# A decoder trunk on one core: softmax rows transposed without scaling, their inverse sums brought through memory into the output gates

## The chip, the cores and the metric

The kernel runs on one core of one Trainium2 chip. The metric is the device time of one execution in microseconds (us). The engines are TensorE (PE: matrix products and transposes), VectorE (DVE), ScalarE (ACT), GpSimd (POOL) and SyncE (SP), whose queue issues nearly all DMA transfers. Each engine works off its own instructions in order and waits for others through semaphores.

## The reference, cut to what matters

The network has two layers on a sequence of 512 tokens with 1024 channels, in float32. Layer 0 mixes tokens with a gated MLP, layer 1 with "forgetting attention"; behind each stands an MLP with squared ReLU. The change is in layer 1's attention:

```python
p = h @ w_in                       # q | k | v | gate | forget logits
q, k = rms_norm(q, q_g), rms_norm(k, k_g)        # per head, 16 heads of 64
c = cumsum(log_sigmoid(f_logit + b_f))           # per head, over tokens
logits = q @ k.T * 64**-0.5 + c[t] - c[s]        # masked to s <= t
probs = softmax(logits)
o = (probs @ v) * sigmoid(gate)
x = x + o @ w_out
```

A softmax row is exp(logit - max) divided by the sum of the row. The division can be made on the row itself, or later on the row's sum of values, since it is one number for each token and head.

## The kernel before, in words

**Products.** Each float32 factor is split into a high part (rounded to the matrix format, by ACT) and a low part (the rest, by DVE or POOL), and a product is three matmuls: high x high, high x low, low x high. Weights come from memory in chunks of up to 512 KB: a raw buffer (three of them), then the split into `wh` (L85, ACT) and `wl` (L86, in the attention stage on POOL). The class `Stream` loads chunks ahead of their use through SP's queue (L80).

**Stages.** The gated MLP layer, its MLP, the attention, the second MLP. The attention runs from about 630 to 922 us of the profile and works on pairs of heads, p = 0 to 7, with head 2p + e and e = 0, 1.

**One pair** is the generator `attend` (L758). The projections `project` (L691) have made q, k and v for all tokens; `attend` turns q and k (L765), scales and splits them (L771 to L775, the low parts on DVE), and then for each of the two heads:

- loads the head's cumulated forget values from memory into all partitions, `cb` (L785, 256 KB, a tag with two buffers), and adds them to the token's own value on POOL: the tiles `bias` (L792, and the causal mask L794), one for each block i of 128 query tokens;
- for i = 0 to 3 makes the negated logits of (i + 1) * 128 keys in PSUM (`lg`), adds the bias and takes the row's minimum on DVE (L803), and takes the exponential with the row's sum `sm` on ACT (L804);
- takes the reciprocal `rc` of the four sums (L806) and scales the four blocks `ee` with it (L808), on DVE.

When both heads are there, and the pair's gates too (`gates[p]`, 128 x 512: the channels of both heads by tokens, from `gate_act`, L729), the blocks are transposed on PE by L840 into PSUM (`tp`), and split into `pth` (ACT, L842) and `ptl` (DVE, L843). `values` (L817) multiplies them with v (PSUM tile `ot`), adds the two halves into `z` (L826 on ACT, L827 on DVE), and multiplies with the gates (L828). The result is split once more (L859, L860) for the output projection.

**What sets the order.** PE's order in the attention stage is written out. The projections of later pairs, the gates and the output products are the main line (`FOX_ORDER`, L35); after each small step of it, `advance` (L866) lets one running `attend` make its next step if its due time has come. A due time is PE time as the program adds it up (`order["us"]`, L239) plus a lag given by the generator at each `yield`: `LAG_SOFT` between the last logits and the first transpose, `LAG_PT` after each set of transposes, and so on. PE's instructions are kept in this order. The instructions of DVE, ACT, POOL and SP are put in order by a scheduler that simulates the whole program; each engine then holds to it. PSUM tiles tagged B (three buffers) serve `lg`, `tp` and the turned q and k alike.

Of the kernel before, what the change touches and what calls it, by code (L numbers as in the profile page):

```python
# [8 lines left out]
F32 = mybir.dt.float32  # L9
F32R = mybir.dt.float32r  # L10
AF = mybir.ActivationFunctionType
ALU = mybir.AluOpType
# [4 lines left out]
P = 128  # L17
D = 1024
S = 512
KB = D // P  # L20
NT = S // P
E = 2 * D
FF = 4 * D
H = 16
DH = 64
# [113 lines left out]
def trunk(ctx: ExitStack, tc: tile.TileContext, A, out, stages=4):  # L139
    nc = tc.nc  # L140
    pe, dve, act, pool = nc.tensor, nc.vector, nc.scalar, nc.gpsimd
# [6 lines left out]
    dram = ctx.enter_context(tc.tile_pool(name="dram", bufs=1, space=DRAM))  # L148
# [4 lines left out]
    def psB(name):  # L153
        return ps.tile([P, S], F32, tag="B", name=name, bufs=3)

    def psD(name):
        return ps.tile([P, S], F32, tag="D", name=name, bufs=1)
# [83 lines left out]
    def mm(dst, a, b, start, stop, more=False):  # L241

        ins = pe.matmul(dst, a, b, start=start, stop=stop, skip_group_check=more)  # L243
        placed(ins, dst.shape[-1])
        return ins

    def turn(dst, src):
        placed(pe.transpose(dst, src, ident[: src.shape[0], : src.shape[0]]), 256)  # L248
# [357 lines left out]
    with ExitStack() as st:  # L606
        fs = st.enter_context(tc.tile_pool(name="fs", bufs=2))
        fp = st.enter_context(tc.tile_pool(name="fp", bufs=2))
# [12 lines left out]
            dve.memset(kl[e][(1 - e) * DH : (2 - e) * DH].bitcast(F32), 0.0)  # L621
        ct = fp.tile([P, NT, H], F32, tag="ct", name="ct", bufs=1)
        cd = dram.tile([H, S], F32, tag="cd", name="cd")

        def forget(pq):

# [30 lines left out]
        gates, vals, o = {}, {}, {}  # L657
# [33 lines left out]
        def project(p, values=True):  # L691
# [33 lines left out]
            pool.tensor_tensor(sf, sf, mhalf, op=ALU.pow)  # L725
            dve.tensor_tensor(yh, yh, sf.unsqueeze(2).to_broadcast([P, NT * 4, DH]), op=ALU.mult)  # L726
            running.append([order["us"] + LAG_NORM, attend(p, y), None])

        def gate_act(p, pg):  # L729
# [28 lines left out]
        def attend(p, y):  # L758

            if p:  # L760
                yield 0.0, ("L", p - 1, 1)
            tq, tk = (psB(f"t{w}{p}") for w in "qk")
            for c, t in enumerate((tq, tk)):
                for i in range(NT):
                    turn(t[:, i * P : (i + 1) * P], y[:, i, c * P : (c + 1) * P])  # L765

            qs, ks = ([fp.tile([P, S], F32R, tag=f"{w}s{e}", name=f"{w}s{p}_{e}") for e in range(2)] for w in "qk")
            own = [slice(0, DH), slice(DH, P)]
            for e in range(2):
                a, b = own[e], own[1 - e]  # L770
                act.activation(qs[e][a], tq[a], AF.Copy, scale=qkn[a])  # L771
                act.activation(ks[e][a], tk[a], AF.Copy, scale=qkg[a, 1:2])
                act.activation(ks[e][b], tk[a], AF.Copy, scale=qkg[a, 1:2])
                dve.scalar_tensor_tensor(qs[e][b], tq[a], qkn[a], qs[e][a].bitcast(F32), op0=ALU.mult, op1=ALU.subtract)
                dve.scalar_tensor_tensor(kl[e][a], tk[a], qkg[a, 1:2], ks[e][a].bitcast(F32), op0=ALU.mult, op1=ALU.subtract)  # L775
            did.add(("Q", p))
            rush = LAST if p > 6 else 1.0
            lag = LAG_QK * rush
            soft = []
            for e in range(2):  # L780
                hd = 2 * p + e
                yield lag, ("T", p - 1, e) if p else "F"
                lag = 0.0
                cb = fp.tile([P, S], F32, tag="cb", name=f"cb{hd}")
                nc.sync.dma_start(cb, cd[hd].partition_broadcast(P))  # L785
                ees = []
                sm = fs.tile([P, NT], F32, tag="sm", name=f"sm{hd}")
                mn = fs.tile([P, NT], F32, tag="mn", name=f"mn{hd}")
                for i in range(NT):
                    n = (i + 1) * P  # L790
                    bi = fp.tile([P, n], F32, tag=f"bias{i}", name=f"bias{hd}_{i}", bufs=1)
                    pool.tensor_scalar(bi, cb[:, :n], 1.0, ct[:, i, hd : hd + 1], op0=ALU.mult, op1=ALU.add)  # L792
                    dg = bi[:, i * P :]
                    pool.affine_select(dg, dg, pattern=[[-1, P]], compare_op=ALU.is_ge, fill=BIG, base=0, channel_multiplier=1)  # L794
                    yield lag, None
                    lag = LAG_LOGIT * rush
                    ee = fp.tile([P, n], F32, tag=f"ee{i}", name=f"ee{hd}_{i}", bufs=2)
                    ees.append(ee)
                    lg = psB(f"lg{hd}_{i}")
                    ts_ = slice(i * P, (i + 1) * P)  # L800
                    mm(lg[:, :n], qs[e][:, ts_], ks[e][:, :n], True, False)
                    mm(lg[:, :n], qs[e][:, ts_], kl[e][:, :n], False, True)
                    dve.tensor_tensor_reduce(ee, lg[:, :n], bi, 1.0, 3.0e38, op0=ALU.add, op1=ALU.min, accum_out=mn[:, i : i + 1])  # L803
                    act.activation(ee, ee, AF.Exp, bias=mn[:, i : i + 1], scale=-1.0, accum_out=sm[:, i : i + 1])  # L804
                rc = fs.tile([P, NT], F32, tag="rc", name=f"rc{hd}")
                dve.reciprocal(rc, sm)  # L806
                for i in range(NT):
                    dve.tensor_scalar(ees[i], ees[i], rc[:, i : i + 1], None, op0=ALU.mult)  # L808
                soft.append(ees)
                did.add(("L", p, e))  # L810
            yield LAG_SOFT * rush, ("G", p)
            if p in (4, 5):
                yield 0.0, ("W", 0)
            weights = []
            z = fp.tile([P, S], F32, tag="oz", name=f"oz{p}")

            def values(e):  # L817

                ot = psD(f"ot{2 * p + e}")
                for j in range(NT):  # L820
                    both = vals[p][:, j, 2 * e : 2 * e + 2].rearrange("p w d -> p (w d)")
                    for w in range(2):
                        mm(ot[:, j * P :], both, weights[e][j][w], j + w == 0, j + w == NT)
                    if j < NT - 1:
                        yield 0.0, None
                act.activation(z[own[e]], ot[own[1 - e]], AF.Copy)  # L826
                dve.tensor_tensor(z[own[e]], ot[own[e]], z[own[e]], op=ALU.add)  # L827
                dve.tensor_tensor(z[own[e]], z[own[e]], gates[p][own[e]], op=ALU.mult)  # L828

            for e in range(2):  # L830
                hd = 2 * p + e
                ph = fp.tile([P, TRI], F32R, tag="pth", name=f"pth{hd}", bufs=2)
                pl = fp.tile([P, TRI], F32R, tag="ptl", name=f"ptl{hd}", bufs=2)
                at = 0
                weights.append([])
                for j in range(NT):
                    n = (NT - j) * P
                    tp = psB(f"tp{hd}_{j}")
                    for i in range(j, NT):
                        turn(tp[:, (i - j) * P : (i - j + 1) * P], soft[e][i][:, j * P : (j + 1) * P])  # L840
                    sl = slice(at, at + n)
                    act.activation(ph[:, sl], tp[:, :n], AF.Copy)  # L842
                    dve.tensor_tensor(pl[:, sl], tp[:, :n], ph[:, sl].bitcast(F32), op=ALU.subtract)  # L843
                    weights[e].append((ph[:, sl], pl[:, sl]))
                    at += n
                    yield LAG_PT * rush, None
                did.add(("T", p, e))
                if e:
                    yield 0.0, ("V", p)
                    yield from values(0)  # L850
                    yield LAG_PV * rush, None
                    yield from values(1)
            if p < 6:
                h = fp.tile([P, S], F32R, tag="oh", name=f"oh{p}", bufs=4)
                l = fp.tile([P, S], F32R, tag="ol", name=f"ol{p}", bufs=4)
            else:
                h = xp.tile([P, S], F32R, tag=f"xh{p}", name=f"oh{p}")
                l = xp.tile([P, S], F32R, tag=f"xl{p}", name=f"ol{p}")
            act.activation(h, z, AF.Copy)  # L859
            dve.tensor_tensor(l, z, h.bitcast(F32), op=ALU.subtract)  # L860
            o[p] = (h, l)
            did.add(("O", p, 1))
# [113 lines left out]
```

## Time and profile before

| | us |
|---|---|
| median of 3 runs | 1277.02 (1276.41 to 1278.97) |
| the profiled execution | 1277.01 |
| its span in the trace | 1275.3 |
| PE busy | 1262.1 (99%) |
| DVE busy | 877.2 (69%) |
| ACT busy | 624.9 (49%) |
| POOL busy | 484.7 (38%) |
| DMA, mean | 97 GB/s |

The span is what the trace covers; the rest of the profiled execution's time lies around it. Busy times are sums over the whole span and hide the stages. A row of a group gives the line, the engine, the operation, the tiles (written <- read), and its times; "idle before" is the time for which the engine stood before the instruction, with what ended it. The granted clock of TensorE was full throughout.

### The profile page before, as it was taken

How to read it: one execution, taken by the hardware profiler on the slowest of the kernel's cores; microseconds unless marked ns; L12 is line 12 of the kernel's file. 1: busy time of each engine (PE TensorE's matmuls, PEld its weight loads, DVE VectorE, ACT ScalarE, POOL GpSimd, SP SyncE). 2: the span in 40 equal slices, each digit the busy share in tenths (PEclk: the TensorE clock that was granted, in tenths of full speed). 3: DMA queues.
4: the chain of work that ended last, by engine and by line, in shares of the span. 5: the costliest groups of instructions: out<-in, count | busy, mean ns of one | idle time of the engine just before them, and what ended most of it. 6: DMA issues, size and time to landing. Idle time of an engine off the chain costs nothing.

```text
span 1275.3 us, 18354 instructions
## 1 busy us (share of the span) xinstructions
PE 1262.1 (99%) x7108; PEld 1114.0 (87%) x7108; DVE 877.2 (69%) x1206; ACT 624.9 (49%) x981; POOL 484.7 (38%) x415
## 2 busy tenths in 40 slices
PE   9999999999999999999999999999999999999998
PEld 7888888888999999998899899898888999999987
DVE  7347767677867676765537777777887767676763
ACT  7334423246534344443467687678465444444430
POOL 4108433025423232310657667667173322323200
PEclk9999999999999999999999999999999999999999
DMA  7333233233233332323223222223223323232321
GB/s 250 97 107 92 83 91 91 84 98 93 90 116 100 100 102 97 111 89 96 80 81 103 84 82 76 84 77 106 83 67 116 116 84 116 84 116 83 118 81 66
DMA packets 39607, 124.01 MB, mean 97 GB/s; under 512 B 4816, under 2 KB 5840, under 8 KB 39520
## 3 DMA queue, kind: packets, MB, share of 16 engines
q1 hardware_dynamic: 39232, 122.82, 30.4%
q8 instruction: 56, 0.92, 0.3%
q14 instruction: 31, 0.25, 0.1%
q10 hardware_dynamic: 288, 0.02, 0.0%
HBM read 120.69 MB, written 2.13 MB: 96 GB/s over the span
## 4 chain that ended last, share of the span: by engine, by line
PE 89%; DVE 6%; ACT 2%; issue 1%; POOL 1%; DMA 1%; DVEq 0%; ACTq 0%; POOLq 0%
PE po L243 36%; PE da L243 11%; PE bc L243 9%; PE pq L243 8%; PE pv L243 8%; PE pu L243 7%; PE ph L243 3%; PE pg L243 2%; PE ot L243 2%; DVE xl L271 1%; PE lg L243 1%; PE tp L248 1%; PE sp L426 1%; DVE ee L808 1%; DVE y L726 1%
## 5 line engine op out<-in xcount | busy, mean ns | idle before, releaser
L85 ACT ACTIVATE wh<-raw 128x1024 fp32r<-128x1024 f32 (+3 forms) x230 | 219.7, 957 | 270.9 <-PE po L243 83.5
L86 DVE TENSOR_TENSOR wl<-raw,wh 128x1024 fp32r<-128x1024 f32 (+1 forms) x178 | 252.5, 1432 | 46.2 <-ACT wh L85 45.4
L243 PE MATMUL po<-zl,wh 128*128 128x512 f32 x512 | 200.6, 392 | 1.3 <-DVE zl L500 1.3
L243 PE MATMUL po<-zh,wh 128*128 128x512 f32 x512 | 199.9, 391 | 0.0
L243 PE MATMUL po<-zh,wl 128*128 128x512 f32 x512 | 199.5, 390 | 0.0
L556 DVE TENSOR_TENSOR x<-x,po 128x512 f32<-128x512 f32 x128 | 87.2, 683 | 106.1 <-PE po L243 106.1
L86 POOL TENSOR_TENSOR wl<-raw,wh 128x768 fp32r<-128x768 f32 (+3 forms) x52 | 102.4, 1969 | 125.7 <-ACT wh L85 123.2
L110 POOL TENSOR_TENSOR ssum<-raw 128x512 f32<-128x512 f32 x26 | 35.5, 1364 | 268.6 <-DMA raw<-in_m_dram 256.8
L85 ACT ACTIVATE sh<-ssum 128x1024 fp32r<-128x1024 f32 x52 | 55.2, 1061 | 164.5 <-POOL ssum L111 95.8
L243 PEld LDWEIGHTS po<-zh,wl 128*128 128x128 f32 x512 | 96.2, 188 | 19.5
L243 PEld LDWEIGHTS po<-zh,wh 128*128 128x128 f32 x512 | 96.5, 188 | 17.9
L243 PEld LDWEIGHTS po<-zl,wh 128*128 128x128 f32 x512 | 96.6, 189 | 17.8 <-DVE zl L500 1.6
L243 PE MATMUL pq<-wh,xh 128*128 128x384 f32 (+2 forms) x256 | 88.4, 345 | 0.0
L410 POOL TENSOR_SCALAR vn<-v,mv,lnr 128x128 f32<-128x128 f32 x64 | 63.1, 999 | 59.5 <-DVE vl L414 59.4
L243 PE MATMUL pq<-wh,xl 128*128 128x384 f32 (+2 forms) x256 | 83.1, 325 | 0.0
L243 PE MATMUL pq<-wl,xh 128*128 128x384 f32 (+2 forms) x256 | 82.7, 323 | 0.0
L86 DVE TENSOR_TENSOR sl<-ssum,sh 128x1024 fp32r<-128x1024 f32 x52 | 65.9, 1268 | 18.2 <-ACT sh L85 18.1
L112 POOL TENSOR_TENSOR ssum<-raw,ssum 128x512 f32<-128x512 f32 x26 | 37.1, 1428 | 69.1 <-DVE sl L86 68.8
L243 PE MATMUL da<-th,sl 128*128 128x256 f32 x208 | 58.9, 283 | 0.0
L243 PE MATMUL da<-tl,sh 128*128 128x256 f32 x208 | 58.8, 283 | 0.0
L243 PE MATMUL pv<-wh,xh 128*128 128x512 f32 (+1 forms) x160 | 58.0, 372 | 0.7 <-ACT wh L85 0.7
L243 PE MATMUL pv<-wl,xh 128*128 128x512 f32 (+1 forms) x160 | 58.7, 368 | 0.0
(212 smaller groups left out, 3489.9 us busy)
## 6 DMA issues: line engine op xcount, KB each, us to landing
raw<-in_m_dram SPq DMA_DIRECT2D x128, 512.0 KB, 3.6
raw<-in_gw_u_dram SPq DMA_DIRECT2D x16, 512.0 KB, 3.5
raw<-in_gw_o_dram SPq DMA_DIRECT2D x16, 512.0 KB, 3.5
raw<-in_fw_qkv_dram SPq DMA_DIRECT2D x20, 384.0 KB, 3.0
raw<-in_gw_v_dram SPq DMA_DIRECT2D x14, 512.0 KB, 3.9
raw<-in_fw_g_dram SPq DMA_DIRECT2D x8, 512.0 KB, 3.4
cb<-cd SPq DMA_DIRECT2D x16, 256.0 KB, 3.3
raw<-in_fw_o_dram SPq DMA_DIRECT2D x8, 512.0 KB, 3.5
```

The source lines that it names most:

```text
L85: self.nc.scalar.activation(hi, t, AF.Copy)
L86: eng.tensor_tensor(lo, t, hi.bitcast(F32), op=ALU.subtract)
L110: tt(s12[:, 0], a21, a22, op=ALU.add)
L112: tt(s43[:, 0], a12, s12[:, 1], op=ALU.subtract)
L243: ins = pe.matmul(dst, a, b, start=start, stop=stop, skip_group_check=more)
L248: placed(pe.transpose(dst, src, ident[: src.shape[0], : src.shape[0]]), 256)
L271: dve.scalar_tensor_tensor(l, x[b], gcol, h.bitcast(F32), op0=ALU.mult, op1=ALU.subtract)
L410: pool.tensor_scalar(vn[:, i], v[i][:, cb * P : (cb + 1) * P], mv[:, i, 0:1], lnr[:, i : i + 1], op0=ALU.subtract, op1=ALU.mult)
L426: pe.matmul(dst, vh[:, 2 * c + i], wide, start=True, stop=False)
L556: dve.tensor_tensor(x[b], x[b], pt, op=ALU.add)
L726: dve.tensor_tensor(yh, yh, sf.unsqueeze(2).to_broadcast([P, NT * 4, DH]), op=ALU.mult)
L808: dve.tensor_scalar(ees[i], ees[i], rc[:, i : i + 1], None, op0=ALU.mult)
```

## The change

The four scalings of a head (L808) go. The blocks are transposed and split as the exponential left them, and the values are summed with these weights. The reciprocals of both heads of a pair are put in one tile `rc` (128 tokens x 2 heads x 4 blocks), and one DMA on SP's queue writes them to memory (`rd`, 16 heads x 512 tokens) so that a head's 512 values lie in a row: 1024 single values of four bytes. After the wait for the pair's gates, two DMAs on SP's queue read the two rows back, each into the 64 partitions of its head: the tile `rb` (128 x 512), which takes its buffers from the tag `cb`. After the transposes of the second head, DVE multiplies the pair's gates with `rb`, and `values` uses these gates as before. No lag is changed.

```diff
+        rd = dram.tile([H, S], F32, tag="rd", name="rd")
...
             soft = []
+            rc = fs.tile([P, 2, NT], F32, tag="rc", name=f"rc{p}")
             for e in range(2):
...
-                rc = fs.tile([P, NT], F32, tag="rc", name=f"rc{hd}")
-                dve.reciprocal(rc, sm)
-                for i in range(NT):
-                    dve.tensor_scalar(ees[i], ees[i], rc[:, i : i + 1], None, op0=ALU.mult)
+                dve.reciprocal(rc[:, e], sm)
                 soft.append(ees)
                 did.add(("L", p, e))
+
+            with nc.allow_non_contiguous_dma(reason="1024 values"):
+                nc.sync.dma_start(rd[2 * p : 2 * p + 2].rearrange("e (i t) -> t e i", t=P), rc)
             yield LAG_SOFT * rush, ("G", p)
+            rb = fp.tile([P, S], F32, tag="cb", name=f"rb{p}")
+            for e in range(2):
+                nc.sync.dma_start(rb[own[e]], rd[2 * p + e].partition_broadcast(DH))
             if p in (4, 5):
                 yield 0.0, ("W", 0)
...
                 did.add(("T", p, e))
                 if e:
+                    dve.tensor_tensor(gates[p], gates[p], rb, op=ALU.mult)
                     yield 0.0, ("V", p)
                     yield from values(0)
```

## The prediction

> **What bounds the kernel now.** The page first: which engine is busy, and what the chain that ended last consists of.
>
> ```profile
> span 1275.3 us, 18354 instructions
> PE 1262.1 (99%) x7108; PEld 1114.0 (87%) x7108; DVE 877.2 (69%) x1206; ACT 624.9 (49%) x981; POOL 484.7 (38%) x415
> ...
> PE 89%; DVE 6%; ACT 2%; issue 1%; POOL 1%; DMA 1%; DVEq 0%; ACTq 0%; POOLq 0%
> ```
>
> TensorE is the bound: 1262.1 of 1275.3 us, and 89% of the chain. Work on DVE counts only where it holds PE up, and DVE is on the chain for 6%. So I looked at the stretch that the change touches, one window for each pair of heads, and at PE's idle time in it: the stretch's length less PE's busy time. (Columns: the window and its length; busy time of PE, weight loads, DVE, ACT and POOL with their instructions; granted clock, share of the DMA engines, GB/s. Eight windows; the four left out are the quiet ones.)
>
> ```profile
> 668.00:698.00 30.00, 29.58 (x182) 28.45 (x182) 21.83 (x49) 21.92 (x49) 22.95 (x28) 1.00 0.35 110
> 698.00:730.00 32.00, 29.42 (x174) 27.18 (x173) 23.57 (x53) 22.64 (x51) 19.95 (x22) 1.00 0.24 71
> ...
> 851.00:878.00 27.00, 26.18 (x191) 24.11 (x189) 21.02 (x47) 21.45 (x46) 18.59 (x23) 1.00 0.29 89
> 878.00:922.00 44.00, 43.37 (x236) 36.41 (x235) 35.41 (x77) 25.34 (x52) 17.50 (x14) 1.00 0.28 91
> sum 254.00, PE 249.27 PEld 226.75 DVE 191.46 ACT 183.07 POOL 159.00; mean PE 31.16 PEld 28.34 DVE 23.93 ACT 22.88 POOL 19.88
> ```
>
> PE idles 254.00 - 249.27 = 4.73 us in the whole stretch, at a granted clock of 1.00. 2.58 of it lie in the second window, 0.82 in the seventh, 0.63 in the last and 0.42 in the first; the other four have 0.3 together. This is the largest part of the argument: however much DVE is relieved, about 4.7 us (0.37%) can come back. PE's ends are modelled, so a little more may hide in "busy"; I allow 1 us.
>
> Then who made PE wait. First PE's waits over the whole trace, next PE's own timeline, then the chain of waits around the same place and one piece of it later on (columns: start, length, what).
>
> ```profile
> PE tp L248 <- DVE ptl L843: 3.6, 4, 1.9
> ```
>
> ```profile
> 714.78 0.30 PE L248 MATMUL tp<-ident,ee 128*128 128x128 f32 x1 [1.87 <-DVE ptl L843]
> ...
> 718.13 0.44 PE L248 MATMUL tp<-ident,ee 128*128 128x128 f32 x2 [0.71 <-DVE ptl L843]
> ```
>
> ```profile
> 681.61 1.08 DVE ee L808 x3
> ...
> 708.18 1.69 DVE ee L808 x3
> ...
> 712.16 1.27 DVE ee L808 x4
> ...
> 715.43 2.44 DVE y L726
> ...
> 864.09 2.42 DVE ee L808 x4
> ```
>
> The transposes' PSUM buffers (three) come free when DVE has made the low part `ptl`, and DVE is late with it since the scalings of L808 stand ahead of it: 1.08 us on the chain in the first window, 1.69 + 1.27 in the second, 2.42 in the seventh. These scalings are what the change removes. Ahead of the second wait (0.71) stands a product of the projections, `y` L726, which stays.
>
> **The change part by part.**
>
> *Removed:* 64 scalings, 8 in each pair. Their busy time over the same eight windows, their durations (least/median/most), and those of the product nearest to what is added:
>
> ```profile
> sum 254.00, DVE 28.64; mean DVE 3.58
> L808 DVE TENSOR_SCALAR ee<-ee,rc x64: 272/470/1510, 674.7 to 895.1; 128x128 f32<-128x128 f32 x16, 128x256 f32<-128x256 f32 x16, 128x384 f32<-128x384 f32 x16, 128x512 f32<-128x512 f32 x16
> L860 DVE TENSOR_TENSOR ol<-oz,oh x8: 683/731/1719, 700.9 to 917.4; 128x512 fp32r<-128x512 f32 x8
> ```
>
> So 28.64 us leave DVE, 3.58 per pair. The 16 reciprocals stay.
>
> *Added on DVE:* 8 products of 128x512 (gates times `rb`). The nearest row is L860, two SBUF inputs of the same shape: 683 ns at least, 731 at the median, 1719 at most. I take 0.73: 5.8 us, bounds 5.5 and 13.8. DVE's net relief is 22.8 us (14.8 to 23.1).
>
> The spread of L808 (272 to 1510 ns) and L860 (683 to 1719) shows DVE instructions being held up now and then. The Trainium skill, page "SBUF — State Buffer", section "Who interferes with whom", has a rule for it: VectorE and GpSimd share one pair of ports, an exclusive lock. By it a product with two SBUF inputs is exposed to POOL's work, so 1.72 rather than 0.73 would be the price: the relief 14.8 and not 22.8 us.
>
> *Moved:* the transposes no longer wait for reciprocal and scaling but for the exponential alone. Their place in PE's order doesn't change: it is written out by the lags, and those are untouched. So a transpose can't start earlier than its turn; only the waits found above can shrink.
>
> *What of the 4.73 us goes.* First window 0.42: 1.08 of scaling is on its chain; gone. Second: the 1.87 goes whole (2.96 us of scaling precede it on DVE), the 0.71 behind `y` L726 by half: 2.2. Seventh: 2.42 us of scaling precede, then other DVE work; half: 0.4. Last: 0.6. Sum 3.6 us. What is late next there is `y` L726 and ACT, which makes the high part.
>
> *Added on the queues:* for each pair one write of 1024 single values (4 KB) to memory and two broadcasts back, 64 partitions of 2 KB each (128 KB). No row shows a write of single values; the nearest DMA rows (KB each, median us from issue to landing):
>
> ```profile
> DMA packets 39607, 124.01 MB, mean 97 GB/s; under 512 B 4816, under 2 KB 5840, under 8 KB 39520
> ...
> cb<-cd SPq DMA_DIRECT2D x16, 256.0 KB, 3.3
> ...
> wsT<-in_w_sT_dram SPq DMA_DIRECT2D x1, 512.0 KB, 3.9
> cd<-cs SPq DMA_DIRECT2D x1, 32.0 KB, 2.0
> ```
>
> `cd<-cs` writes 16 rows in 2.0 us, the lower bound. `wsT` moves 128 x 8 rows of 512 B (the 5840 - 4816 = 1024 packets between the two sizes) in 3.9: as many packets as the new write has, only far fuller; the upper bound. I take 3.0. The two broadcasts together move what one `cb<-cd` moves in 3.3, and the second issue adds an estimated 0.4; below, the 2.0 of the small write, and 0.4. I take 3.0. From the last reciprocal of a pair, R, the sums are back at R + 6.0 us (4.4 to 7.6, the sums of the bounds).
>
> *Who waits for them.* The product waits on DVE, in order; behind it stand the `ptl` of the transposes and the next pair's work, and PE waits for these. The pair at 742 us on DVE:
>
> ```profile
> 743.40 0.18 DVE L806 RECIPROCAL rc<-sm 128x4 f32<-128x4 f32 x1 [0.64 <-ACT ee L804]
> ...
> 749.03 1.72 DVE L843 TENSOR_TENSOR ptl<-tp,pth 128x512 fp32r<-128x512 f32 x4 [0.42 <-ACT pth L842]
> 754.64 0.68 DVE L827 TENSOR_TENSOR oz<-ot,oz 64x512 f32<-64x512 f32 x1 [3.89 <-ACT oz L826]
> 755.36 0.68 DVE L828 TENSOR_TENSOR oz<-oz,gt 64x512 f32<-64x512 f32 x1
> ```
>
> R is 743.6. The gates are needed at 755.4, R + 11.8, and DVE idles from 750.7 to 754.6, R + 7.2 to R + 11.1. In program order the product comes right behind that last `ptl`: the sums (R + 6.0) are there, and the product lies in the hole and costs nothing. If DVE's order has it earlier, where the scheduler thought the sums were back, DVE stands for a microsecond or two with `ptl` behind it. PE's idle time per DVE time has been 4.73 / 28.64 = 0.17; 8 pairs x 0.5 us x 0.17 = 0.7 us lost. I take 0.5.
>
> The Trainium skill, page "DMA: Bandwidth & Descriptors", section "Specifications", speaks against this write: below 512 B a transfer does read-modify-write. If that doubles what `wsT` takes above the 2.0 us of the small write, the new one takes 5.8 us, 2.8 more than I took, and if all of it were DVE standing, the sum would be 8 x 2.8 x 0.17 = 3.8 us higher, 1277.7 us: the gain gone. No row of before shows such a write, and the hole of 3.9 us covers the 2.8; 0.04 of the chance of "nothing to be measured" (below) is for it.
>
> *SP.* Its queue stands waiting most of the time, each load for a buffer:
>
> ```profile
> SPq L80 <- POOL wl L86: 188.7, 39, 7.1
> ```
>
> A write put behind such a load comes later, by 188.7 / 39 = 4.8 us on average; a load put behind the write or the broadcasts comes later by the 3.0 us for which the broadcasts wait. The weights are three raw buffers ahead of their use, and PE's waits name no load; I cost it at nothing. Without that cover it is 3 us in a pair, 24 in all.
>
> **Sum.** The profiled execution took 1277.01 us (span 1275.3 and 1.7 around it), the median of the runs is 1277.02: the same. 1277.0 - 3.6 + 0.5 = 1273.9 us, -0.24%. About 0.2% (2.6 us) is what a measurement of this kernel can tell from no change, so the forecast is only just "faster".
>
> **The rivals.**
>
> *B, nothing to be measured.* PE's order is fixed and four of eight windows have no idle time to give. If ACT and `y` L726 are late anyway, only the 1.87 shrinks, by half, and the first 0.42 goes: 1277.0 - 1.4 = 1275.6. For it: the 0.71 stands behind `y`. Against it: 2.96 us of scaling stand ahead of a wait of 1.87.
>
> *C, slower: the sums come late, and DVE stands at the product.* In SP's order the write gets behind a load that waits 4.8 us; back at R + 10.8 while DVE came to it at R + 6. The rate: at 3.58 us of scaling per window, DVE's lateness cost PE 2.58 in the second window and 0.3 in each of the others. 4.8 us per pair then costs 0.4 to 3.5; in the middle 1.9, 8 pairs 15.5 us: 1277.0 - 3.6 + 15.5 = 1289 (1277 to 1301). With half the pairs hit, 1281. It decides from 3.58 - 0.73 = 2.9 us of standing per pair, where DVE loses what it gained. For it: SP's waits, and the unseen write of single values. Against: the hole of 3.89 us, and 4.4 to 7.6 against 11.8.
>
> *D, the forget rows come late.* `rb` shares the two buffers of `cb`, so the second head's `cb` of the next pair can load only once the product is done, 3.3 us before its first use. Tightest here (POOL, then DVE):
>
> ```profile
> 820.87 0.37 POOL L792 TENSOR_SCALAR bias<-cb,ct 128x128 f32<-128x128 f32 x1
> ```
>
> ```profile
> 827.63 0.28 DVE L803 CUSTOM_DVE_ANT_0 ee<-lg,bias 128x128 f32<-128x128 f32 x1
> ```
>
> That pair's last `ptl` ends near 822; product 822.7, `cb` landed 826.0, bias 0.7 later: 0.9 us before DVE wants it at 827.63. Each microsecond beyond that is PE's once three buffers of logits are full. With the sums 2 us late in all seven pairs that have a successor, about 1 us each: 1273.9 + 7 = 1281.
>
> **Chances.** The forecast 0.50 (its own range 1271.3, all 4.73 and 1 more gone, to 1275.5), B 0.27, C 0.16, D 0.07. Of the forecast 0.42 lie below 1274.5 and 0.08 above; B is "same", C and D "slower". So faster 0.42, same 0.35, slower 0.23. The range reaches below to 1270.5 and above to 1284, into C.
>
> **What would show it.** Right: PE's wait for `ptl` falls from 3.6 us to under 1, PE's idle time in the stretch to 1 to 2 us, DVE loses some 23 us, and no wait of DVE on a DMA `rb` over 1 us. The write lands in 2.0 to 3.9 us. Wrong: a row of DVE waiting for `rb` with several microseconds (C); POOL waiting for `cb` (D); DVE 23 us lighter with PE's idle time as before (B).

## The result and the profile after

The changed kernel takes 1360.97 us at the median of four executions (three of 1360.18 to 1361.32 and a disturbed one of 6354.67; without that one the median is 1360.62), the kernel before 1277.18 in the same job. The ratio, without the disturbed execution, is 1.0652, interval 1.0631 to 1.0673: 83.8 us slower by the medians, where 3.1 us faster was forecast. The profiled execution took 1360.18 us.

The page of the kernel after, the same lines as before:

```profile
span 1358.4 us, 18347 instructions
PE 1279.0 (94%) x7108; PEld 1129.7 (83%) x7108; DVE 854.7 (63%) x1150; ACT 624.6 (46%) x981; POOL 484.3 (36%) x415
...
PE 79%; DMA 7%; DVE 5%; issue 3%; ACT 2%; POOL 2%; SPq 0%; DVEq 0%; POOLq 0%; ACTq 0%
```

The span grew by 83.1 us. PE's idle time went from 1275.3 - 1262.1 = 13.2 to 1358.4 - 1279.0 = 79.4 us, 66.2 more; its busy time grew by 16.9 for the same 7108 matmuls. 66.2 + 16.9 = 83.1: the whole loss, in two parts. DMA, 1% of the chain before, is now 7%. DVE is 22.5 us lighter (877.2 to 854.7), as meant.

The waits of the attention stage (who waited <- for whom: us in all, how often, longest), and the DMA issues of the tiles concerned (KB each, median us from issue to landing):

```profile
DVE gt L854 <- DMA rb<-rd: 76.0, 8, 10.7
POOL bias L794 <- DMA cb<-cd: 73.6, 8, 10.5
...
PE tp L248 <- DVE ptl L848: 62.5, 10, 9.6
...
PE pq L243 <- DVE x L325: 9.2, 1, 9.2
```

```profile
cb<-cd SPq DMA_DIRECT2D x16, 256.0 KB, 3.8
...
rb<-rd SPq DMA_DIRECT2D x16, 128.0 KB, 4.6
...
rd<-rc SPq DMA_DIRECT2D x8, 4.0 KB, 9.0
```

DVE stands at the new product in all eight pairs, 9.5 us on average, and PE stands behind it: 62.5 us for a `ptl`, where it was 3.6, and in the fifth pair 9.2 us for an `x` (L325), which DVE makes right behind the product there. The write of 4 KB takes 9.0 us to land at the median, longer than any other transfer here; the loads of 64 times its size take 3.8. The first pair on DVE, and then the chain of waits at the same place:

```profile
680.39 0.18 DVE L807 RECIPROCAL rc<-sm 128x4 f32<-128x4 f32 x1 [0.62 <-ACT ee L806]
...
683.50 0.88 DVE L848 TENSOR_TENSOR ptl<-tp,pth 128x384 fp32r<-128x384 f32 x2
694.30 0.69 DVE L854 TENSOR_TENSOR gt<-gt,rb 128x512 f32<-128x512 f32 x1 [9.92 <-DMA rb<-rd]
694.91 0.88 DVE L848 TENSOR_TENSOR ptl<-tp,pth 128x128 fp32r<-128x128 f32 x2
```

```profile
680.60 9.34 DMA rd<-rc
689.95 0.51 SPq L816
690.51 3.69 DMA rb<-rd
694.30 0.69 DVE gt L854
695.25 0.69 PE tp L248 x2
```

The last reciprocal ends at R = 680.57. The sums are back at 694.2, R + 13.6. DVE's order has the product after three of the eight `ptl`, at R + 3.8 (684.38), with five `ptl` of the same pair behind it. PE needs these to free its PSUM buffers, so it stands too. In the other pairs the product comes after none to four of the eight.

What PE does around that stall (columns as in the prediction; the granted clock comes after the engines):

```profile
684.40:694.30 9.90, 1.90 (x14) 1.54 (x12) 0.00 (x0) 2.01 (x3) 2.17 (x1) 0.73 0.23 54
689.10:699.10 10.00, 3.85 (x13) 3.75 (x14) 3.69 (x7) 0.66 (x2) 3.55 (x5) 0.50 0.43 118
699.30:726.00 26.70, 24.77 (x145) 22.82 (x144) 17.64 (x38) 20.01 (x45) 17.38 (x18) 1.00 0.23 65
```

While DVE stands (first row, DVE 0.00) PE finds 1.90 us of work. In the second row the granted clock is 0.50 for 10 us; PE starts again at 695.25 and does 3.85 us of matmuls in it at half speed, of which about half, 1.9, is lost. There is such a stretch of half clock in each of the eight pairs, and PE is busy for 36.6 us in all of them together; half of that, 18.3 us, is close to the 16.9 by which PE's busy time grew. From 699.3 the clock is 1.00 again. The Trainium skill, page "TensorE: Matmul & The Clock Gate", Part 1, says that the gate goes back to half speed after about 3.4 us of idling and opens after as long a busy time; the trace agrees roughly: the granted clock is half from 689.0, 2.7 us after PE's last matmul (it ends at 686.3), and full again from 699.2, 4.0 us after PE's restart. It is full throughout the attention of the kernel before, whose longest wait for a `ptl` was 1.9 us.

### The profile page after: what moved, and what is told of

Same layout as the page of the kernel before. It is cut to its first block, busy times and chain, and to the rows that moved or that the text cites. A ratio compares the mean times of both kernels' runs of the same rounds, so it can differ in the third digit from the quotient of the medians.

```text
span 1358.4 us, 18347 instructions
## 1 busy us (share of the span) xinstructions
PE 1279.0 (94%) x7108; PEld 1129.7 (83%) x7108; DVE 854.7 (63%) x1150; ACT 624.6 (46%) x981; POOL 484.3 (36%) x415
## 4 chain that ended last, share of the span: by engine, by line
PE 79%; DMA 7%; DVE 5%; issue 3%; ACT 2%; POOL 2%; SPq 0%; DVEq 0%; POOLq 0%; ACTq 0%
PE po L243 32%; PE da L243 11%; PE bc L243 8%; PE pv L243 7%; PE pu L243 6%; PE pq L243 6%; DMA rd<-rc 5%; PE ph L243 2%; DMA rb<-rd 2%; PE pg L243 2%; DVE xl L271 1%; PE ot L243 1%; POOL wl L86 1%; PE lg L243 1%; PE sp L426 1%
## 5 line engine op out<-in xcount | busy, mean ns | idle before, releaser
L243 PE MATMUL pq<-wh,xh 128*128 128x384 f32 (+2 forms) x256 | 92.2, 360 | 9.2 <-DVE x L325 9.2
L248 PE MATMUL tp<-ident,ee 128*128 128x128 f32 x160 | 32.2, 303 | 62.5 <-DVE ptl L848 62.5
L243 PE MATMUL pq<-wh,xl 128*128 128x384 f32 (+2 forms) x256 | 86.1, 336 | 0.0
L243 PE MATMUL pq<-wl,xh 128*128 128x384 f32 (+2 forms) x256 | 86.0, 336 | 0.0
L248 PEld LDWEIGHTS tp<-ident,ee 128*128 128x128 f32 x160 | 22.4, 154 | 70.2 <-DVE ptl L848 66.1
L794 POOL TENSOR_SCALAR bias<-cb,ct 128x128 f32<-128x128 f32 (+1 forms) x64 | 38.9, 618 | 83.5 <-DMA cb<-cd 73.6
L847 ACT ACTIVATE pth<-tp 128x512 fp32r<-128x512 f32 (+1 forms) x64 | 27.2, 433 | 87.9 <-PE tp L248 87.8
```

## The experiments

**Theory 1:** the scattered write is slow, DVE stands at the product for it, in order, ahead of the `ptl` that PE needs. **Theory 2:** the transfers hurt without the product: `rb` takes a buffer of `cb`, and the broadcasts stand in SP's queue waiting for the write, so the forget rows come late (73.6 us of POOL waiting for `cb`). The first three runs tell these apart.

### No inverse at all

```diff
-            with nc.allow_non_contiguous_dma(reason="1024 values"):
-                nc.sync.dma_start(rd[2 * p : 2 * p + 2].rearrange("e (i t) -> t e i", t=P), rc)
...
-            rb = fp.tile([P, S], F32, tag="cb", name=f"rb{p}")
-            for e in range(2):
-                nc.sync.dma_start(rb[own[e]], rd[2 * p + e].partition_broadcast(DH))
...
-                    dve.tensor_tensor(gates[p], gates[p], rb, op=ALU.mult)
```

> The changed kernel without the write of the inverse sums, their way back and the product with the gates: the division by the rows' sums is left out, so this is the ceiling of what the missing scalings can bring. By the forecast's term (3.6 us of PE's idle time come back, nothing added): 1273.4 us, PE's wait for ptl under 1 us. By rival B (ACT and the product y are late anyway): 1275.6 us. If the missing scalings themselves disturbed the order: above 1277.

Measured: 1275.01 us (1272.10 to 1276.53), ratio 0.9977 (0.9968 to 0.9986). Removing the scalings alone is worth 2.2 us; 3.6 was forecast. PE's waits for `ptl` are not shorter than the 3.6 us of before, and a long `y` product of the projections stands where the scalings were (waits, then DVE's timeline; the profiled execution took 1276.37 us):

```profile
PE tp L248 <- DVE ptl L841: 4.1, 3, 2.2
```

```profile
712.55 3.34 DVE L726 TENSOR_TENSOR y<-y,yss 128x1024 f32<-128x1024 f32 x1
```

So 27.6 us less work on DVE (877.2 to 849.6) buys 2.2; the 83.8 us come from what is added, not from what the transposes now carry.

### The transfers without the product

```diff
-                    dve.tensor_tensor(gates[p], gates[p], rb, op=ALU.mult)
```

> The changed kernel with the write and both broadcasts, but without the product: the division is left out. Theory 1 (DVE stands at the product, 76 us, with ptl behind it, and PE behind that): without the product nothing of DVE waits for the sums, so 1274 to 1280 us, and PE's wait for ptl falls from 62.5 to under 3 us. Theory 2 (SP's queue stands for the write, and the forget rows cb come late behind it and in the shared buffers: POOL waits 73.6 us for them): the wait of POOL stays over 50 us and the time stays above 1320 us.

Measured: 1294.21 us, ratio 1.0132 (1.0119 to 1.0146). Neither theory alone. The product with its standing is 1360.97 - 1294.21 = 66.8 us; the transfers by themselves cost 1294.21 - 1275.01 = 19.2. The waits, and SP's queue in the first pair:

```profile
POOL bias L794 <- DMA cb<-cd: 71.3, 8, 10.4
...
PE lg L243 <- DVE mn L805: 8.9, 2, 5.7
...
PE tp L248 <- DVE ptl L848: 7.2, 3, 3.8
```

```profile
680.55 0.38 SPq L812 DMA_DIRECT2D rd<-rc  x1
689.45 1.15 SPq L816 DMA_DIRECT2D rb<-rd  x2
690.65 0.58 SPq L787 DMA_DIRECT2D cb<-cd  x1
```

The broadcasts wait on SP until the write has landed (680.55 to 689.45), and the load of the next forget rows stands behind them. POOL's `bias` comes late by up to 10.4 us, and with it the logits.

### The same 4 KB as 128 rows

The write keeps its 4 KB, its place and everything behind it, but each partition's eight values go out side by side (32 bytes). They come back in another order, so this kernel has all the work but not the right division.

```diff
-            with nc.allow_non_contiguous_dma(reason="1024 values"):
-                nc.sync.dma_start(rd[2 * p : 2 * p + 2].rearrange("e (i t) -> t e i", t=P), rc)
+            nc.sync.dma_start(rd[2 * p : 2 * p + 2].rearrange("e s -> (e s)").rearrange("(t w) -> t w", t=P), rc.rearrange("p e i -> p (e i)"))
```

> The changed kernel, but the 4 KB are written as 128 rows of 32 bytes in place of 1024 single values; the way back reads the same 4 KB, so the values land in another order (the division goes wrong, all work is there). If the number of single values makes the write slow (9.0 us): it lands in 2 to 3 us, the sums are back some 6.5 us earlier, DVE's wait at the product falls from 76 to about 25 us, and the time to 1285 to 1300 us. If it is the way through memory as such: it lands in 8 to 9 us and the time stays at 1361.

Measured: 1286.08 us (1282.59 to 1286.86), ratio 1.0063 (1.0049 to 1.0077). DMA issues and waits, in an execution of 1282.59 us:

```profile
rb<-rd SPq DMA_DIRECT2D x16, 128.0 KB, 2.9
...
rd<-rc SPq DMA_DIRECT2D x8, 4.0 KB, 2.2
```

```profile
POOL bias L794 <- DMA cb<-cd: 18.5, 7, 4.2
...
DVE gt L853 <- DMA rb<-rd: 11.4, 7, 2.9
...
PE tp L248 <- DVE ptl L847: 9.2, 10, 1.9
```

The form of the write is 1360.97 - 1286.08 = 74.9 of the 83.8 us. The broadcasts land sooner with it too, after 2.9 us where they took 4.6, though nothing of their own was changed; why isn't shown. The rest stays: even with a write of 2.2 us, inside the prediction's bounds of 2.0 to 3.9, the kernel is slower than before, with DVE's order unchanged: DVE stands at the product for 11.4 us in all, and POOL 18.5 us for forget rows that are late behind the broadcasts. How the rest divides between the two isn't shown.

### The forms of the write by themselves

Behind the last output of the kernel before stands a chain of small DMAs, each waiting for the one ahead. It ran once.

```diff
+        nc.sync.dma_start(row(d[0]).rearrange("(t w) -> t w", t=P), s[0])
...
+        nc.sync.dma_start(d[1].rearrange("w t -> t w"), s[1])
...
+        nc.sync.dma_start(d[2][:4].rearrange("w t -> t w"), s[2][:, :4])
...
+        nc.sync.dma_start(d[3][:1].rearrange("w t -> t w"), s[3][:, :1])
...
+        nc.sync.dma_start(d[4][:, :1].rearrange("(t w) o -> t (w o)", t=P), s[5])
```

> The kernel before, and behind its last output a chain of small DMAs, each waiting for the one before, to measure landing times by themselves: writes of 1024, 512 and 128 single values side by side, of 1024 single values 512 bytes apart, of 128 rows of 32 bytes, and reads of 1024 single values. If each single value costs the write something: 9, 5.5 and 2.9 us (2.0 and 7 us for 1024), and 9 for the values 512 bytes apart. If it is neighbours in one piece of memory that hold each other up: the values 512 bytes apart land in 2 to 4 us. Reads of 1024 single values: 3 to 4 us (data packets alone), or 9 if reads pay as writes do. Rows of 32 bytes: 2 to 2.5.

Measured, issue to landing: 128 rows of 32 bytes 1.7 us; 1024 single values side by side in memory 10.6, 512 of them 10.4, 128 of them 7.2; 1024 single values 512 bytes apart 2.8. Reads of 1024 single values: 2.1 side by side, 2.6 when 512 bytes apart. So it is neither the number of pieces nor their size that costs, but that single values are written beside each other. The issue of the 10.6 us write and the next one, and the DMA engines in between (last two columns: their share, GB/s):

```profile
1276.70 0.37 SPq L912 DMA_DIRECT2D d<-m  x1
1287.40 0.32 SPq L913 DMA_DIRECT2D m<-d  x1
```

```profile
1276.70:1278.70 2.00, 0.00 (x0) 0.00 (x0) 0.00 (x0) 0.00 (x0) 0.00 (x0) 0.50 0.23 2
1278.70:1287.30 8.60, 0.00 (x0) 0.00 (x0) 0.00 (x0) 0.00 (x0) 0.00 (x0) 0.50 0.00 0
```

The DMA engines show work in the first 2 us alone; for 8.6 us nothing moves on them, and the write still isn't reported as landed. The Trainium skill, page "DMA: Bandwidth & Descriptors", section "Anatomy of one DMA", says of DMAs issued by GpSimd that one is reported only when the memory has confirmed its last byte; these rows, of DMAs on SP's queue, agree with that.

### How near the values stand

The same chain with 1024 single values at other distances, also run once.

```diff
+    wide = {n: dram.tile([1024, n], F32, tag=f"d{n}", name=f"d{n}") for n in (64, 16, 8, 2)}
+    at = lambda n: wide[n][:, :1].rearrange("(t w) o -> t (w o)", t=P)
...
+        nc.sync.dma_start(own, s[5].rearrange("g (a o) -> g a o", o=2)[:, :, 0])
```

> As the chain of small DMAs behind the last output of the kernel before, now with 1024 single values 256, 64, 32 and 8 bytes apart, and last 1024 values side by side of which each run of 64 (256 bytes) comes from one partition. Theory: single values written by different DMA engines into one small piece of memory wait for each other. 256 and 64 bytes apart: 2.5 to 3.5 us, as 512 bytes apart (2.85); 8 bytes apart: 6 to 11 us, as side by side (10.6); 32 bytes apart tells the size of the piece. Runs of 64 from one partition: 2.5 to 4 us if only different engines disturb each other; 5 to 8 if neighbours do whoever writes them.

| 1024 single values | us to landing |
|---|---|
| 256 bytes apart | 3.0 |
| 64 bytes apart | 3.1 |
| 32 bytes apart | 4.5 |
| 8 bytes apart | 5.8 |
| side by side, 64 from each of 16 partitions | 9.0 |
| side by side, neighbours from 128 partitions (run before) | 10.6 |

Nothing is lost down to 64 bytes; below, the time grows as more values share 64 bytes, though not in proportion. It doesn't need two partitions to write there: neighbours from one partition cost nearly as much. What in the way to memory holds them up isn't shown.

### Buffers of its own for `rb`

```diff
-            rb = fp.tile([P, S], F32, tag="cb", name=f"rb{p}")
+            rb = small.tile([P, S], F32, tag="sqs", name=f"rb{p}", bufs=2)
```

> The changed kernel with one edit: the returned sums rb have two buffers of their own (those of the norms' partial sums, idle in this stage) and no longer share those of the forget rows cb. If the 19 us by which the kernel without the product stays above the one without any inverse sums come from the shared buffers: POOL's wait for cb falls from 73.6 to under 10 us and the time falls by 10 to 20 us from 1361, to 1340 to 1350; DVE's stand at the product stays at some 75 us, since the write still lands after 9 us. If they come from SP's queue standing for the write: POOL's wait stays above 40 us and the time near 1361.

Measured: 1361.85 us, ratio 1.0659 (1.0642 to 1.0675): no gain, a miss. The waits and SP's queue:

```profile
DVE gt L854 <- DMA rb<-rd: 74.3, 8, 10.7
...
POOL bias L794 <- DMA cb<-cd: 4.5, 1, 4.5
```

```profile
680.48 0.33 SPq L787 DMA_DIRECT2D cb<-cd  x1
680.86 0.43 SPq L812 DMA_DIRECT2D rd<-rc  x1
689.48 1.15 SPq L816 DMA_DIRECT2D rb<-rd  x2
```

With its own buffer the load of `cb` goes out at 680.48, ahead of the write, and POOL's wait falls from 73.6 to 4.5 us. The time doesn't move: while DVE stands at the product, forget rows that come late cost nothing. The two costs overlap, so the 19.2 us of the transfers can't be added to the product's. How much of the 19.2 is the shared buffers and how much SP's queue isn't separated: no run has buffers of its own without the product.

### The slow write, its use late

The write stays as it is. `rb` has its own buffers, the broadcasts are held back behind the second head's `ptl` (by a small memset of `rb` pinned there), and not the gates but the finished sums are multiplied with `rb`, pinned behind the second head's values. Of the pair's work that PE waits for, only the last split for the output projection still comes after it.

```diff
-                dve.tensor_tensor(z[own[e]], z[own[e]], gates[p][own[e]], op=ALU.mult)
...
+                    tc.keep_in_program_order(dve.memset(rb[:, :2], 0.0))
+                    for c in range(2):
+                        nc.sync.dma_start(rb[own[c]], rd[2 * p + c].partition_broadcast(DH))
...
                     yield from values(1)
+                    dve.tensor_tensor(z, z, gates[p], op=ALU.mult)
+                    tc.keep_in_program_order(dve.tensor_tensor(z, z, rb, op=ALU.mult))
```

> The changed kernel with the slow write kept, but nothing early waits for it: rb has its own buffers, the broadcasts wait for the end of the second head's transposes (a small memset on DVE ahead of them), and the product with rb comes last on the pair, behind the second head's values, on the whole z (the gates' product too, so two products of 128x512 take the place of two of 64x512 and one of 128x512). The sums are wanted 18 us after the reciprocal and return after some 14. Theory (the write itself harms nobody, only who waits for it): DVE's wait for rb under 5 us in all, POOL's wait for cb under 10, 1274.5 to 1277 us. If 1024 neighbouring single values also slow other transfers or engines: above 1280.

Measured: 1275.91 us (1273.38 to 1276.98), ratio 0.9985 (0.9977 to 0.9994): 1.3 us faster than the kernel before in the same job and far faster than the changed one, with a write that takes 9.5 us. DMA, the new product's group (columns: busy us in all, mean ns of one, then the idle time before it), and PE's waits:

```profile
rd<-rc SPq DMA_DIRECT2D x8, 4.0 KB, 9.5
```

```profile
L859 DVE TENSOR_TENSOR oz<-oz,rb 128x512 f32<-128x512 f32 x8 | 6.4, 801 | 0.0
```

```profile
PE tp L248 <- DVE ptl L845: 2.7, 4, 1.4
```

The idle time ahead of the product is 0.0 in all eight pairs. So the slow write is the cause only together with the place where its result is used. The run moves the buffers and the broadcasts too; buffers alone changed nothing (the run before).

### A fast write, its use late

As the last, but `rc` is transposed on PE, copied by ACT and written as eight rows of 512 bytes.

```diff
+                    turn(rt[:8, :P], rc.rearrange("p e i -> p (e i)"))
+                    act.activation(rs[:8, :P], rt[:8, :P], AF.Copy)
+                    nc.sync.dma_start(rd[2 * p : 2 * p + 2].rearrange("e (i t) -> (e i) t", t=P), rs[:8, :P])
```

> As the late product, but the 128 x 8 inverse sums are transposed by PE (one more transpose for a pair) and copied by ACT, so that the write is 8 rows of 512 bytes. Theory (neighbouring single values make the write slow): it lands in 1.4 to 2 us, as the rows of 32 bytes did; sums back some 6 us after the reciprocal; 1275 to 1277 us, 0.9 us of PE more than the late product at most.

Measured: 1276.71 us, ratio 0.9997 (0.9988 to 1.0005). SP waits at most 1.5 us for a write now, and nothing is won by it: the broadcasts were early enough with the slow one, and the transposes and copies are work of their own.

### The product alone

The product stands at its place in the program, but with ones from SBUF; no write, no broadcast; the division is left out. DVE's order doesn't keep that place: the first product runs at 645.87, 35 us ahead of the first pair's last reciprocal, where the changed kernel has it at 694.30.

```diff
-                    dve.tensor_tensor(gates[p], gates[p], rb, op=ALU.mult)
+                    gv = gates[p].rearrange("p (i t) -> p i t", t=P)
+                    dve.tensor_tensor(gv, gv, ones.unsqueeze(1).to_broadcast([P, NT, P]), op=ALU.mult)
```

> The changed kernel without the write and the way back: the product with the gates is there, but with ones (the division is left out). The price of the eight products alone: by the forecast's term 5.8 us of DVE's time, 0.5 to 1 us of the whole, so 1275.5 to 1276; DVE's products 0.69 us each as measured in the changed kernel. Below 1275 or above 1277.5 the term was mis-sized.

Measured: 1278.73 us (1276.97 to 1280.81), ratio 1.0011 (1.0002 to 1.0020), 3.7 us above the kernel without inverse. A miss of the small price that I had for it. PE's waits for `ptl` rose from 4.1 to 6.5 us:

```profile
PE tp L248 <- DVE ptl L841: 6.5, 5, 2.8
```

So eight products of this size can eat the gain of removing the scalings even when nothing is waited for. Three of them took 1.39 to 1.77 us, where all eight took 0.69 in the changed kernel. The run says nothing of the place behind the third `ptl`. PE's longest wait, 2.8 us at 717.08, follows a product at 716.01 that stands ahead of three `ptl`, but without the product the wait there was 2.2 already, and the rest of the 3.7 us isn't accounted for.

### The `y` product in halves

The late product, and the long `y` product cut in two, to see whether it holds back what is missing of the 3.6 us.

```diff
+            for c in range(2):
+                yc = slice(8 * c, 8 * c + 8)
+                dve.tensor_tensor(yh[:, yc], yh[:, yc], sf[:, yc].unsqueeze(2).to_broadcast([P, 8, DH]), op=ALU.mult)
```

> The late product with one more edit: the product y of the projections (128x1024, two SBUF inputs, L726 of before), which took 1.30 us in the late product's profile but 3.34 us at the same place without the inverse sums, is made in two halves of 512, so that a ptl can come between them. If y is what is late next behind the missing scalings: PE's wait for ptl falls from 2.7 us to under 1.5 and the time by 1 to 2 us, to 1274 to 1275. If it is ACT's high part: no change against 1275.9.

Measured: 1276.71 us (1276.11 to 1277.83), ratio 1.0000 (0.9991 to 1.0009). A miss; `y` isn't shown to be the next limit, and why 2.2 and not 3.6 us came stays open.

## Why the prediction was wrong

**The write's landing: the first step that failed.** I took 3.0 us, with 2.0 and 3.9 as bounds from `cd<-cs` and `wsT`. It took 9.0. Both rows were the wrong kin: one writes 16 long rows, the other reads; neither writes single values beside each other. Full rows and reads don't share this cost (1.7 and 2.1 us for the same 4 KB), so the upper bound wasn't one. The rule of the Trainium skill that I weighed (page "DMA: Bandwidth & Descriptors", section "Specifications"), of read-modify-write below 512 bytes, pointed the right way, but the 5.8 us that I estimated by it were too few, and its limit isn't what decides here: rows of 32 bytes took 1.7 us, single values 64 bytes apart 3.1.

**The broadcasts** took 4.6 us each at the median, and 4.25 both together in the first pair (689.95 to 694.20), not 3.0 (at most 3.7): a mis-sized term, and one that hangs on the write, since behind rows they took 2.9 each. The sums were back at R + 13.6 in the first pair, not R + 6.0 (4.4 to 7.6).

**The product's place: the second step that failed.** "Right behind that last `ptl`" is program order; DVE's order is made by a scheduler, and it put the product at R + 3.8, ahead of five `ptl`. I had named that possibility and priced it at a microsecond or two of standing. This error alone would have lost the gain: with a write of 2.2 us at this place the kernel takes 1286.08. The other alone probably too: in the hole that I expected, R + 7.2 to R + 11.1, sums back at R + 13.6 would still make DVE stand for about 2.5 us a pair (worked out, not run).

**The rate at which DVE's standing reaches PE** I took as 0.17, from short delays that PE's buffers absorbed. Here it is 66.2 / 76.0 = 0.87. After 1.90 us of work PE has nothing left, and of a stall of 9.5 us all but that goes through. A rate measured on stalls shorter than the cover says nothing of longer ones.

**The half clock**, some 17 us, stood in no term.

**The product itself** I took as hidden in DVE's hole, with 0.5 us for a wrong place. With ones, and nothing to wait for, it cost 3.7 us (1278.73 against 1275.01).

**SP and the buffers.** "I cost it at nothing" was wrong: bare, the transfers cost 19.2 us, near the 24 that I named without cover, though not through the weights but through `cb` behind the broadcasts, which is rival D's wait (POOL for `cb`, 73.6 us). In the changed kernel it is hidden by DVE's standing.

**The rivals.** C is the mechanism that decided: DVE standing at the product for late sums, with just the sign named for it (a wait of DVE for `rb`). Its reason, the write behind a load on SP, was another one: the write went out at once and landed late. Its sum also had DVE at the product at R + 6, where the hole of the same prediction runs from R + 7.2 to R + 11.1: sums back at R + 10.8 would have been in time. Its size, 4.8 us a pair at a rate of 0.1 to 0.7 and so 1289 us, fell 72 us short. My range ended at 1284.

**What held.** DVE lost 22.5 us (22.8 said); the new product takes 0.69 us (0.73 said); the ceiling on the gain is small, 2.2 us measured without the added work against 3.6 said and 4.73 at most. Its make-up didn't hold: the wait of 1.87 us that was to go whole is 2.2 us long without the scalings, with the long `y` (3.34 us) ahead of it.

## What to carry to other kernels

Price a transfer by a row with the same shape on the side that is written: single values side by side in memory are no cousin of rows. Before calling an instruction that waits for a DMA hidden, find its place in its engine's own order, not in the program, and look at what stands behind it; if the order isn't yours, pin it behind the work that others wait for. The same slow write cost 84 us with its use ahead of that work, and nothing with its use, the broadcasts too, behind it.

## What the runs showed of the hardware

- A DMA that writes 1024 single float32 values side by side to memory lands after 8.7 to 9.5 us at the median of a kernel's eight and 10.6 alone, there with the DMA engines idle for 8.6 of it; 128 values alone already take 7.2. At 64 bytes apart or more 1024 values take 2.8 to 3.1, as rows of 32 bytes 1.4 and 1.7 alone (2.2 at the median in the kernel), and reads of the same single values take 2.1 to 2.6.
- A stall of PE of 9 us is paid twice: once as idle time, and again as some 1.9 us for the half clock that lasts for about the first 4 us of running (695.25 to 699.2 in the first pair; 18.3 us over the eight stalls).
